# A float32 encoder trunk on one core: first two weight units by residual tile, row factors with tokens on partitions, last unit by token halves

## The chip, the cores and the metric

The kernel runs on one core of a Trainium2 chip. The metric is the device time of one execution in microseconds; where several runs are compared, their median is taken. The engines are named as in the profile: PE multiplies matrices (PEld is its loading of weights), DVE, ACT and POOL work elementwise, SP issues DMA transfers.

## The reference

A trunk of two layers on 512 tokens with 1024 features, in float32. Each layer adds four steps to the residual stream h; the mixer is a bidirectional Mamba-2 scan (SSD) in the first layer and a two-dimensional neighbourhood attention in the second.

```python
def rmsnorm(x, g):
    xf = x.astype(jnp.float32)
    y = xf * lax.rsqrt(jnp.mean(xf * xf, axis=-1, keepdims=True) + RMS_EPS)
    return (y * g.astype(jnp.float32)).astype(x.dtype)

def swiglu(x, w_gu, w_down):
    g, u = jnp.split(x @ w_gu, 2, axis=-1)
    return (jax.nn.silu(g) * u) @ w_down

for i in range(DEPTH):
    h = h + 0.5 * swiglu(rmsnorm(h, ffn1_norm[i]), ffn1_w_gu[i], ffn1_w_down[i])
    hn = rmsnorm(h, mix_norm[i])
    h = h + (ssd_mixer(hn, ...) if i % 2 == 0 else neighbourhood_attention(hn, ...))
    h = h + 0.5 * swiglu(rmsnorm(h, ffn2_norm[i]), ffn2_w_gu[i], ffn2_w_down[i])
    gate = jax.nn.sigmoid(rmsnorm(h, ple_norm[i]) @ ple_w_gate[i])
    h = h + gate * rmsnorm(p[i] @ ple_w_proj[i], ple_post_norm[i])
```

The hidden width of a feed-forward is 2816, the scan has eight groups of four heads, and the SSD mixer norms its inner 2048 features once more before its output product.

## The kernel before

**Data.** The residual lies on chip as eight tiles `h[k]` (named `hs`) of 128 features x 512 tokens, features on the partitions. Every weight matrix is cut into *units* of 128 output features: a tile `wr` of 128 x 1024. Since PE works faster on a shortened form of float32 (fp32r), each operand is split exactly into a high and a low part: `load_unit` (L149) issues a unit's transfer on SP, `split_unit` casts the high part `wh` on ACT (L157) and subtracts the low part `wl` on DVE (L159). Transfers run in the order of `plan()`, with four `wr` buffers and three of each part, so about three units stand ready ahead of use. The tiles of the residual are split likewise into pairs (`xa`, in the feed-forward after the mixer `md`): ACT L181 makes h * gain, DVE L182 its low part.

**Product.** `gemm` makes a unit's product in one PSUM bank (`ps`, 128 x 512): for each of the eight residual tiles three matmuls, high by high (L172), high by low (L173), low by high (L174), 24 in all.

**Norm.** The root-mean-square factor of a token is not applied to the input but to the product. `SumSq.add` squares a tile on ACT (L201) and adds it on POOL (L205; the eighth on DVE). `SumSq.rsqrt` multiplies the sum `acc` by a matrix of 1/1024 (L209), so that the sum over features stands on all 128 partitions, and DVE makes 1/sqrt of it on 128 x 512 (L211, then L187, L188 and three Newton steps L191 to L193) into a tile `rt`. This happens 11 times: in each layer for the two feed-forwards, the mixer, the embedding's projection and the embedding's gate, and once for the inner norm of the SSD. The calls stand behind the first unit, or the first two, that need the factor.

**Stages.** `ffn` makes gate and up units in chunks of 8, 7 and 7, each followed by `down` products of the chunk before, which add to the residual (L267); in the last `down` each finished tile is prepared for the next norm at once. In the second feed-forward `ple_proj` runs between; its `finish`, called after the third tile of the last `down`, makes a factor and scales eight tiles by it (L312). `ple` multiplies eight gate units and updates the residual (L326 to L330). In `ssd`, groups of heads are projected and scanned alternately; at its end the output products (L608, L609, L613) are scaled by the factor of the inner norm. `attention` begins with the keys.

**Order.** The instructions of each engine run in a fixed order that a scheduler made from the program when it was built. At the start of the trunk (L837 on) the constants, the eight tiles of x and the first units are issued on SP; tiles and two units are then split, and the squares counted.

Of the kernel before, what the change touches and what calls it, by code (L numbers as in the profile page):

```python
# [14 lines left out]
P = 128  # L15
T = 512
# [12 lines left out]
# columns of the packed per-partition constants  # L29
# [7 lines left out]
# columns of the shape-only constants  # L37
# [8 lines left out]
def trunk(ctx, tc, A, out):  # L46
# [45 lines left out]
    s.activation(out=warm, in_=ones_d[:, 0:1], func=AF.Silu)  # L92
# [5 lines left out]
    def park(k):  # L98
        """The residual leaves the chip while a mixer runs."""
        hd = dp.tile([P, T], F32, name=nm("hd"))  # L100
        sy.dma_start(out=hd, in_=h[k])
        h[k] = None
        return hd
# [63 lines left out]
    def gemm(pt, w, pairs, first=True, last=True, off=0):  # L167
        hi, lo = w
        n = len(pairs)
        for k, xp in enumerate(pairs):  # L170
            sl = slice((off + k) * P, (off + k + 1) * P)
            te.matmul(out=pt, lhsT=hi[:, sl], rhs=xp[:, 0, :], start=first and k == 0, stop=False)  # L172
            te.matmul(out=pt, lhsT=hi[:, sl], rhs=xp[:, 1, :], start=False, stop=False)  # L173
            te.matmul(out=pt, lhsT=lo[:, sl], rhs=xp[:, 0, :], start=False, stop=last and k == n - 1)  # L174

    def split(dst, src, gain):
        if gain is None:
            s.copy(out=dst[:, 0, :], in_=src)  # L178
            v.tensor_sub(out=dst[:, 1, :], in0=src, in1=dst[:, 0, :])
        else:  # L180
            s.activation(out=dst[:, 0, :], in_=src, func=AF.Copy, scale=gain)  # L181
            v.scalar_tensor_tensor(out=dst[:, 1, :], in0=src, scalar=gain, in1=dst[:, 0, :],  # L182
                                   op0=ALU.mult, op1=ALU.subtract)

    def newton_rsqrt(m, y, a):
        """y = 1 / sqrt(m) on VectorE: a first guess from the bits of m and three Newton steps."""
# [8 lines left out]
    class SumSq:  # L195
# [11 lines left out]
        def rsqrt(self, scale=1.0, eps=EPS):  # L207
            pt = px_bank()
            te.matmul(out=pt, lhsT=ones_d, rhs=self.acc, start=True, stop=True)  # L209
            m, a, y = sc(), sc(), rt()  # L210
            v.tensor_scalar(out=m, in0=pt, scalar1=scale, scalar2=eps, op0=ALU.mult, op1=ALU.add)  # L211
            newton_rsqrt(m, y, a)
            return y

    class Norm:
        """RMSNorm of the residual: the pairs carry h * gain, the row factor is applied after the product."""
# [7 lines left out]
        def prep(self, k, count=True):  # L224
            pr = self.alloc()
            split(pr, h[k], col(self.gain + k))
            self.pairs.append(pr)
            if count:
                self.count(k)
# [4 lines left out]
        def factor(self, half=False):  # L234
            if half:
                return self.ss.rsqrt(4.0, 4.0 * EPS)
            return self.ss.rsqrt()

# [1 line left out]
    def ffn(norm, nxt, between=lambda: None):  # L240
# [3 lines left out]
        def gate_up(f):  # L244
            pg = mm_bank()
            gemm(pg, unit(), norm.pairs)
            pu = mm_bank()
            gemm(pu, unit(), norm.pairs)
            if R[0] is None:
                R[0] = norm.factor()  # L250
# [11 lines left out]
        def down(c, finish=None):  # L262
            a, b = CHUNKS[c]
            for d in range(KD):
# [5 lines left out]
                if d == 2 and finish is not None:  # L270
                    finish()
# [14 lines left out]
    def ple_proj(l):  # L286
# [22 lines left out]
        def finish():  # L309
            r3 = ss.rsqrt(4.0, 4.0 * EPS)  # L310
# [4 lines left out]
        return pp, finish  # L315

    def ple(l, norm, pp, nxt):
        R = None
        for n in range(KD):
            pt = mm_bank()  # L320
            gemm(pt, unit(), norm.pairs)
            if R is None:
                R = norm.factor(half=True)
            u = t2()
            for cs in ((slice(0, T),) if n < KD - 1 else (slice(0, T // 2), slice(T // 2, T))):
                v.tensor_mul(out=u[:, cs], in0=pt[:, cs], in1=R[:, cs])  # L326
                s.activation(out=u[:, cs], in_=u[:, cs], func=AF.Tanh)
                v.scalar_tensor_tensor(out=u[:, cs], in0=u[:, cs], scalar=1.0, in1=pp[n][:, cs],
                                       op0=ALU.add, op1=ALU.mult)
                v.tensor_add(out=h[n][:, cs], in0=h[n][:, cs], in1=u[:, cs])  # L330
            nxt(n)

# [1 line left out]
    def ssd(norm, nxt):  # L334
# [4 lines left out]
        s.activation(out=ea, in_=ea, func=AF.Exp)  # L339
# [6 lines left out]
        R = norm.factor()  # L346
# [14 lines left out]
        def steps():  # L361
            """Step sizes, tokens on the partitions, and their running sums."""
# [6 lines left out]
            # softplus(z) = max(z, 0) + 2 atanh(e / (2 + e)), e = exp(-|z|)  # L369
# [56 lines left out]
        def project(gi):  # L426
# [3 lines left out]
            for i in range(8):  # L430
                pt = mm_bank()
                gemm(pt, unit(), norm.pairs)
# [18 lines left out]
        def scan(gi, bt, ct_, xt, zt):  # L451
            """One group of heads, in steps: what a step's products need was made in the steps before."""
            h0 = 4 * gi
            # masked C B^T of each direction, keys on the partitions
# [10 lines left out]
            # token-major xs and B  # L465
# [24 lines left out]
            def decay(hd):  # L490
                es = []
                for dr in range(2):
# [3 lines left out]
                    # the exponents of masked entries are held at 0  # L496
# [10 lines left out]
            # states carried from chunk to chunk  # L507
# [20 lines left out]
            # outputs, two heads to a tile  # L528
# [71 lines left out]
        r2 = ss.rsqrt(0.5)  # L600
        prs = pairs_of(range(8, 16), lambda: md(F32R))
        for d in range(KD):
            pt = mm_bank()
            gemm(pt, unit(), prs)
# [5 lines left out]
            # from here on tokens go column by column of the grid, so that every window of the attention is one run  # L610
# [7 lines left out]
    def attention(norm, nxt):  # L618
# [3 lines left out]
        kz = []  # L622
        R = None

        def keys(js):
            """Keys of four head pairs, normalised."""
# [3 lines left out]
            for j in js:  # L630
                pt = mm_bank()
                gemm(pt, unit(), norm.pairs)
                if R is None:
                    R = norm.factor()
# [23 lines left out]
        def stack_keys(j):  # L658
            """For each head its high parts twice over and its low parts twice over."""
# [12 lines left out]
        def stack_queries(qb):  # L672
            """For each head its high parts over its low parts, in the order of its keys' rows."""
# [14 lines left out]
        def project(j):  # L688
            """Queries and values of a head pair, in four steps."""
# [35 lines left out]
        def attend(j):  # L725
            """The four query blocks of a head pair: scores, then weights, then values, one step apart."""
# [111 lines left out]
    sy.dma_start(out=cst[:, :C_GM], in_=A["cst"][:, :C_GM])  # L838
    for k in range(KD):
        sy.dma_start(out=h[k], in_=A["x"][:, k, :])  # L840
        if k in (1, 3):
            load_unit()
# [3 lines left out]
    for k in range(KD):  # L846
        n.prep(k, False)
        if k in (1, 3):
            split_unit()
    for k in range(KD):  # L850
        n.count(k)
    for i in range(stop):
# [4 lines left out]
        if w == 0:  # L857
            ffn(n, nxt)
# [9 lines left out]
def prepare(inp):  # L868
# [62 lines left out]
    # the relative position bias laid out by query (row, column) and key (row, column)  # L931
# [29 lines left out]
```

## Time and profile before

| | us |
|---|---|
| median of 3 runs | 2466.24 |
| lowest and highest run | 2465.31, 2467.89 |
| span of the profiled execution, first to last instruction | 2462.0 |
| PE busy in it | 2395.0 (97%) |
| DVE busy | 1548.6 (63%) |
| ACT busy | 964.0 (39%) |
| POOL busy | 489.4 (20%) |

The profile shows one execution; for it the span is given, and the runs' times are those of whole executions. A row of a timeline reads: start, duration, engine, line, operation, output <- input, shape, count, and in brackets the idle time of the engine just before and what ended it. A row of the waits reads: waiting engine, tile and line, what released it, then total us, times, longest. A row of a window reads: the stretch, its length, busy time and (in brackets) instruction count of PE, PEld, DVE, ACT and POOL, then the granted clock of PE as a share of full speed, the busy share of the DMA engines and GB/s. A group of instructions reads: count, total us and mean ns of one. Starts of successive matmuls tell PE's pace; their durations overlap.

### The profile page before, as it was taken

What the parts mean: (1) busy time and instruction counts of PE and PEld (TensorE: products, weight loads), DVE (VectorE), ACT (ScalarE), POOL (GpSimd) and SP (SyncE); (2) the same over time, 40 slices, a digit from 0 to 9 for tenths busy, and PEclk for the clock granted to TensorE, in tenths of its full rate; (3) what the DMA queues carried; (4) which work ended last, traced back from release to release, by engine and by line L of the source; (5) the groups of instructions that cost most, each with busy time, mean ns of one, the idle gap of its engine ahead of it and who ended that gap; (6) DMA issues with size and microseconds to landing.
All of it is one profiled execution on the core that took longest, in us unless ns stands there. A gap on an engine that the chain in (4) does not pass through costs nothing. (4 is left out here: it accounts for less than half of the span.)

```text
span 2462.0 us, 29096 instructions
## 1 busy us (share of the span) xinstructions
PE 2395.0 (97%) x11278; PEld 1953.4 (79%) x11278; DVE 1548.6 (63%) x1983; ACT 964.0 (39%) x1545; POOL 489.4 (20%) x387
## 2 busy tenths in 40 slices
PE   8999999999999999899999999999999999999998
PEld 6888888777777778788888778888877878888887
DVE  6553448888888866645344964444478965553457
ACT  4322234555555563332234432222336753322242
POOL 2110110545555543211012111101100011110120
PEclk9999999999999999999999999999999999999999
DMA  4333342533443354233333333333434323333332
GB/s 165 96 96 100 90 126 89 167 119 122 125 123 120 122 174 129 87 101 94 96 102 95 95 93 99 99 94 92 139 120 125 112 67 99 96 94 99 99 94 77
DMA packets 89562, 266.60 MB, mean 108 GB/s; under 512 B 10944, under 2 KB 11584, under 8 KB 89424
## 3 DMA queue, kind: packets, MB, share of 16 engines
q1 hardware_dynamic: 89424, 264.75, 35.5%
q8 instruction: 88, 1.44, 0.2%
q14 instruction: 50, 0.41, 0.1%
HBM read 253.93 MB, written 10.78 MB: 108 GB/s over the span
## 5 line engine op out<-in xcount | busy, mean ns | idle before, releaser
L172 PE MATMUL ps<-xa,wh 128*128 128x512 f32 x2216 | 877.9, 396 | 17.9 <-ACT xa L181 9.2
L173 PE MATMUL ps<-xa,wh 128*128 128x512 f32 x2216 | 870.7, 393 | 3.3 <-DVE xa L182 3.3
L174 PE MATMUL ps<-xa,wl 128*128 128x512 f32 x2216 | 869.1, 392 | 0.0
L157 ACT CAST wh<-wr 128x1024 fp32r<-128x1024 f32 (+1 forms) x405 | 418.4, 1033 | 1027.2 <-PE ps L173 638.8
L159 DVE TENSOR_TENSOR wl<-wr,wh 128x1024 fp32r<-128x1024 f32 (+1 forms) x405 | 588.8, 1454 | 126.4 <-ACT wh L157 121.0
L172 PEld LDWEIGHTS ps<-xa,wh 128*128 128x128 f32 x2216 | 419.7, 189 | 108.0 <-ACT xa L181 10.6
L173 PEld LDWEIGHTS ps<-xa,wh 128*128 128x128 f32 x2216 | 419.7, 189 | 97.2 <-issue 7.1
L174 PEld LDWEIGHTS ps<-xa,wl 128*128 128x128 f32 x2216 | 418.9, 189 | 88.5 <-DVE wl L159 1.2
L172 PE MATMUL ps<-md,wh 128*128 128x512 f32 x960 | 376.6, 392 | 1.2 <-ACT md L181 1.2
L173 PE MATMUL ps<-md,wh 128*128 128x512 f32 x960 | 374.0, 390 | 1.1 <-DVE md L182 1.1
L174 PE MATMUL ps<-md,wl 128*128 128x512 f32 x960 | 373.5, 389 | 0.0
L257 POOL TENSOR_TENSOR t<-t,sc 128x512 f32<-128x512 f32 x88 | 121.2, 1379 | 1025.4 <-ACT wh L157 735.0
L205 POOL TENSOR_TENSOR sq<-sq,sq 128x512 f32<-128x512 f32 x77 | 112.0, 1454 | 595.8 <-ACT sq L201 594.6
L256 DVE TENSOR_TENSOR t<-ps,rt 128x512 f32<-128x512 f32 x88 | 60.8, 690 | 255.5 <-PE ps L174 255.5
L172 PEld LDWEIGHTS ps<-md,wh 128*128 128x128 f32 x960 | 180.2, 188 | 41.2 <-ACT md L181 2.4
L173 PEld LDWEIGHTS ps<-md,wh 128*128 128x128 f32 x960 | 180.2, 188 | 40.4 <-DVE md L182 2.3
L267 DVE SCALAR_TENSOR_TENSOR hs<-ps,hs 128x512 f32<-128x512 f32 x96 | 66.2, 690 | 229.7 <-PE ps L174 229.7
L174 PEld LDWEIGHTS ps<-md,wl 128*128 128x128 f32 x960 | 180.2, 188 | 37.6
L420 DVE SCALAR_TENSOR_TENSOR t<-t,ccw,t 128x510 f32<-128x510 f32 (+1 forms) x192 | 178.8, 934 | 5.3 <-ACT t L416 2.8
L252 DVE TENSOR_TENSOR t<-ps,rt 128x512 f32<-128x512 f32 x88 | 60.8, 691 | 127.4 <-PE ps L174 127.2
L501 POOL TENSOR_TENSOR sc<-sc,sc 128x512 f32<-128x512 f32 x64 | 106.7, 1688 | 29.8 <-ACT sc L500 29.8
L178 ACT CAST md<-t 128x512 fp32r<-128x512 f32 x88 | 54.9, 624 | 120.5 <-POOL t L257 120.5
(154 smaller groups left out, 1771.3 us busy)
## 6 DMA issues: line engine op xcount, KB each, us to landing
wr<-in_w_gu_dram SPq DMA_DIRECT2D x176, 512.0 KB, 3.6
wr<-in_w_in_dram SPq DMA_DIRECT2D x65, 512.0 KB, 3.6
wr<-in_w_dn_dram SPq DMA_DIRECT2D x64, 448.0 KB, 3.3
wr<-in_w_dn_dram SPq DMA_DIRECT2D x32, 512.0 KB, 3.5
hs<-crow SPq DMA_DIRECT2D x64, 256.0 KB, 3.6
wr<-in_w_qkv_dram SPq DMA_DIRECT2D x24, 512.0 KB, 3.6
hs<-vrow SPq DMA_DIRECT2D x64, 128.0 KB, 3.0
wr<-in_w_out_dram SPq DMA_DIRECT2D x16, 512.0 KB, 4.0
```

The lines of the kernel that those rows point to most:

```text
L157: s.copy(out=hi[:, :n], in_=raw[:, :n])
L159: v.tensor_sub(out=lo[:, :n], in0=raw[:, :n], in1=hi[:, :n])
L172: te.matmul(out=pt, lhsT=hi[:, sl], rhs=xp[:, 0, :], start=first and k == 0, stop=False)
L173: te.matmul(out=pt, lhsT=hi[:, sl], rhs=xp[:, 1, :], start=False, stop=False)
L174: te.matmul(out=pt, lhsT=lo[:, sl], rhs=xp[:, 0, :], start=False, stop=last and k == n - 1)
L205: (v if fast else g).tensor_add(out=self.acc, in0=self.acc, in1=q)
L252: v.tensor_mul(out=gm, in0=pg, in1=R[0])
L256: v.tensor_mul(out=um, in0=pu, in1=R[0])
L257: g.tensor_mul(out=um, in0=um, in1=sg)
L267: v.scalar_tensor_tensor(out=h[d], in0=pt, scalar=0.5, in1=h[d], op0=ALU.mult, op1=ALU.add)
L420: v.scalar_tensor_tensor(out=a[:, lo:hi], in0=xb[:, lo + o:hi + o], scalar=w(j), in1=a[:, lo:hi], op0=ALU.mult, op1=ALU.add)
L501: g.tensor_mul(out=e, in0=e, in1=cbm[dr])
```

## The change

*Row factor.* It is made in two parts. `begin` multiplies, for each block of 128 tokens, the squares as weights with one column of ones, so that the sums of 128 tokens stand on 128 partitions; 1/sqrt is made by DVE on 128 x 4. `end` broadcasts each column of factors as weights and multiplies it by the identity, which brings the factors into rows on all partitions, and ACT copies them to `rt`.

```diff
-        def rsqrt(self, scale=1.0, eps=EPS):
+        def begin(self, scale=1.0, eps=EPS):
             pt = px_bank()
-            te.matmul(out=pt, lhsT=ones_d, rhs=self.acc, start=True, stop=True)
-            m, a, y = sc(), sc(), rt()
-            v.tensor_scalar(out=m, in0=pt, scalar1=scale, scalar2=eps, op0=ALU.mult, op1=ALU.add)
-            newton_rsqrt(m, y, a)
-            return y
+            for c in range(NC):
+                te.matmul(out=pt[:, c:c + 1], lhsT=self.acc[:, c * P:(c + 1) * P], rhs=ones_d[:, :1],
+                          start=True, stop=True)
+            m, a, self.y = sm([NC]), sm([NC]), sm([NC])
+            v.tensor_scalar(out=m, in0=pt[:, :NC], scalar1=scale, scalar2=eps, op0=ALU.mult, op1=ALU.add)
+            newton_rsqrt(m, self.y, a)
+
+        def end(self):
+            pt = px_bank()
+            for c in range(NC):
+                te.matmul(out=pt[:, c * P:(c + 1) * P], lhsT=self.y[:, c:c + 1].to_broadcast([P, P]), rhs=ident,
+                          start=True, stop=True)
+            r = rt()
+            s.copy(out=r, in_=pt)
+            return r
```

Between the two parts lies a unit's product: in `ffn` the up unit, in `ple` the second unit (the first one's result is held in its bank till then), in `ssd` the first unit of group 0, in `attention` a second unit of keys, made ahead, in the SSD's output stage the first and second unit. `ple_proj` hands two calls to `down`, after its second and its third tile.

```diff
             pt = mm_bank()
             gemm(pt, unit(), norm.pairs)
-            if R is None:
-                R = norm.factor(half=True)
...
+            if n == 0:
+                norm.begin(half=True)
+                held = pt
+                continue
+            if n == 1:
+                R = norm.end()
+                gate(0, held, R, slice(0, T))
+                nxt(0)
```

*Start.* The constants and, in halves of 512 columns, the first two units are issued on ACT's queue; the halves are cast behind tile 0 and tile 3. The first feed-forward's gate and up products go side by side, residual tile by tile. All squares come after the last cast of a residual tile. The table of the exponential for the SSD's decay rates is used later (`ea` is kept in program order).

```diff
+    sy.dma_start(out=h[0], in_=A["x"][:, 0, :])
+    s.dma_start(out=cst[:, :C_GM], in_=A["cst"][:, :C_GM])
+    for x in range(2):
+        for src, raw, hi, lo in begun:
+            s.dma_start(out=raw[:, wcols[x]], in_=src[:, wcols[x]])
+    s.activation(out=warm, in_=ones_d[:, 0:1], func=AF.Silu)
...
     for k in range(KD):
         n.prep(k, False)
-        if k in (1, 3):
-            split_unit()
-    for k in range(KD):
-        n.count(k)
+        if k in (0, 3):
+            for src, raw, hi, lo in begun:
+                sl = wcols[k // 3]
+                s.copy(out=hi[:, sl], in_=raw[:, sl])
+                last_lo = v.tensor_sub(out=lo[:, sl], in0=raw[:, sl], in1=hi[:, sl])
+
+    def first(pg, pu, pairs):
+        for k in range(KD):
+            for pt, (src, raw, hi, lo) in zip((pg, pu), begun):
+                gemm(pt, (hi, lo), pairs[k:k + 1], first=k == 0, last=k == KD - 1, off=k)
+
+        with tc.issue_after(n.last_cast.ins):
+            for k in range(KD):
+                n.count(k)
```

*Tail.* The last gate unit of the last layer is multiplied in two halves of 256 tokens, each in a bank of its own; each half is gated and its residual stored at once, one on SP's queue and one on ACT's. Before, one product was gated in two halves.

```diff
+            if n == KD - 1 and nxt is done:
+                w = unit()
+                for x, cs in enumerate(halves):
+                    pt = mm_bank()
+                    gemm(pt[:, cs], w, norm.pairs, cols=cs)
+                    gate(n, pt[:, cs], R, cs)
+                    (sy, s)[x].dma_start(out=out[:, n, cs], in_=h[n][:, cs])
+                continue
```

How the change moves instructions, at three places. In the changed kernel `gemm` has the lines 171 to 173, the casts are at L156 and L921, their subtractions at L158, the tiles' casts at L180 and L181, `begin` at L211 and L214, `end` at L221 and L224; `ps_140` is the gate's and `ps_141` the up unit's bank.

PE at the start of the program, before (the first rows, and those where the second unit begins):

```order
L172 MATMUL ps_159<-xa_100,wh_108 128x512
L173 MATMUL ps_159<-xa_100,wh_108 128x512
L174 MATMUL ps_159<-xa_100,wl_110 128x512
...
L172 MATMUL ps_159<-xa_124,wh_108 128x512
L172 MATMUL ps_190<-xa_100,wh_120 128x512
L173 MATMUL ps_190<-xa_100,wh_120 128x512
L173 MATMUL ps_159<-xa_124,wh_108 128x512
```

and after the change:

```order
L171 MATMUL ps_140<-xa_108,wh_83 128x512
L172 MATMUL ps_140<-xa_108,wh_83 128x512
L173 MATMUL ps_140<-xa_108,wl_84 128x512
L171 MATMUL ps_141<-xa_108,wh_86 128x512
L172 MATMUL ps_141<-xa_108,wh_86 128x512
L173 MATMUL ps_141<-xa_108,wl_87 128x512
L171 MATMUL ps_140<-xa_115,wh_83 128x512
```

The first bank was filled nearly to its end before the second one began; now the two alternate with every residual tile.

PE at the end of these two units in the changed kernel (`sq_190` is the sum of squares, `sm_220` the factors, `ps_250` the third unit's bank):

```order
L173 MATMUL ps_141<-xa_137,wl_87 128x512
L211 MATMUL ps_213<-ones_d,sq_190 128x1 x4
...
L171 MATMUL ps_250<-xa_134,wh_253 128x512
L221 MATMUL ps_233<-msk,sm_220 128x128 x4
L172 MATMUL ps_250<-xa_134,wh_253 128x512
```

The first part of the factor stands behind both units, the second part inside the third.

DVE where the last `down` of the first layer's second feed-forward meets the embedding's projection, before (`hs` with L267 is a residual tile's update, L182 its low part, L312 the scaling):

```order
L267 SCALAR_TENSOR_TENSOR hs_7679<-ps_10183,hs_7679 128x512
L192 SCALAR_TENSOR_TENSOR sc_10126<-sc_10126,sc_10125 128x512
L159 TENSOR_TENSOR wl_10223<-wr_10089,wh_10221 128x896
L193 SCALAR_TENSOR_TENSOR rt_10127<-sc_10126,rt_10127 128x512
L182 SCALAR_TENSOR_TENSOR md_10212<-hs_7679,cst,md_10212 128x512
L312 SCALAR_TENSOR_TENSOR xa_9929<-xa_9929,cst,rt_10127 128x512 x2
L312 SCALAR_TENSOR_TENSOR xa_9951<-xa_9951,cst,rt_10127 128x512 x2
L312 SCALAR_TENSOR_TENSOR xa_9980<-xa_9980,cst,rt_10127 128x512 x2
L312 SCALAR_TENSOR_TENSOR xa_10003<-xa_10003,cst,rt_10127 128x512 x2
L267 SCALAR_TENSOR_TENSOR hs_7723<-ps_10218,hs_7723 128x512
L159 TENSOR_TENSOR wl_10258<-wr_10149,wh_10256 128x1024
L182 SCALAR_TENSOR_TENSOR md_10247<-hs_7723,cst,md_10247 128x512
```

and after, from the last Newton step of the factor on (L290 is the update, L335 the scaling):

```order
L191 TENSOR_TENSOR sm_10138<-sm_10139 128x4
L192 SCALAR_TENSOR_TENSOR sm_10138<-sm_10138,sm_10137 128x4
L193 SCALAR_TENSOR_TENSOR sm_10139<-sm_10138,sm_10139 128x4
L290 SCALAR_TENSOR_TENSOR hs_7656<-ps_10152,hs_7656 128x512
L158 TENSOR_TENSOR wl_10207<-wr_10098,wh_10205 128x896
L181 SCALAR_TENSOR_TENSOR md_10181<-hs_7656,cst,md_10181 128x512
L335 SCALAR_TENSOR_TENSOR xa_9973<-xa_9973,cst,rt_10192 128x512 x2
L335 SCALAR_TENSOR_TENSOR xa_9995<-xa_9995,cst,rt_10192 128x512 x2
L335 SCALAR_TENSOR_TENSOR xa_10024<-xa_10024,cst,rt_10192 128x512 x2
L335 SCALAR_TENSOR_TENSOR xa_10047<-xa_10047,cst,rt_10192 128x512 x2
L290 SCALAR_TENSOR_TENSOR hs_7700<-ps_10202,hs_7700 128x512
L158 TENSOR_TENSOR wl_10242<-wr_10153,wh_10240 128x896
```

The scaling stood behind the low part of `hs_7679` and stands one tile earlier now (`hs_7700` answers to `hs_7679` of before); the factor's operations have 128x4 elements instead of 128x512 and stand closer together.

117 lines of the change are left out of this document (75 added, 42 removed).

## The prediction

> **What bounds the kernel now.** I read the page's table of engines first, then the waits of PE, then the timeline at each place that the change touches.
>
> ```profile
> span 2462.0 us, 29096 instructions
> PE 2395.0 (97%) x11278; PEld 1953.4 (79%) x11278; DVE 1548.6 (63%) x1983; ACT 964.0 (39%) x1545; POOL 489.4 (20%) x387
> PE ps L556 <- DVE md L526: 23.0, 14, 2.0
> ...
> PE ps L172 <- ACT xa L181: 9.2, 4, 4.5
> PE ps L172 <- ACT wh L157: 8.7, 1, 8.7
> PE ps L173 <- DVE xa L182: 3.3, 5, 1.3
> PE ps L172 <- ACT md L181: 1.2, 2, 0.6
> PE ps L173 <- DVE md L182: 1.1, 2, 0.5
> ```
>
> PE is busy 97% of the span, so a change gains only where it takes matmul time away or closes one of PE's gaps. The waits name the gaps. The largest, 23.0 us, lies inside the groups of the SSD scan, whose instructions the change leaves in their order (so does a second one there, on POOL). The rest is at the start (8.7 us before the first matmul, 3.3 us at L173) and where one stage hands over to the next (9.2, 1.2 and 1.1 us). The change can win there, some 15 us at most, and it pays for it with more instructions on PE.
>
> **The row factor.** It is made 11 times. Before, one fp32 matmul of the all-ones matrix with the squares (L209) gives the sum to all partitions, and twelve DVE operations run on 128x512.
>
> ```profile
> 380.44 1.02 PE L209 MATMUL ps<-sq,ones_d 128*128 128x512 f32 x2
> ...
> 381.53 0.39 PE L173 MATMUL ps<-xa,wh 128*128 128x512 f32 x1
> 381.76 0.40 PE L174 MATMUL ps<-xa,wl 128*128 128x512 f32 x1
> 1881.75 1.09 PE ps L711 x8
> L711 PE MATMUL ps<-msk,sc 128*128 128x128 f32 x64 | 8.7, 279 | 0.0
> L366 PE MATMUL ps<-msk,t x4: 222/222/272, 397.8 to 398.0; 64*128 64x64 f32 x4
> L209 PEld LDWEIGHTS ps<-sq,ones_d 128*128 128x128 f32 x22 | 4.0, 188 | 1.4 <-PE ps L173 0.4 <-DVE sq L205 0.3
> ```
>
> Steady matmuls start .23 us apart (381.53, 381.76). L209 starts at 380.44 and the second matmul behind it at 381.53: 1.09 less one matmul's .23 is .86 us of PE that goes. In its place come two pieces. The second piece (four matmuls with a column of factors broadcast as weights and the identity streamed, eight instructions, since fp32 runs as two) has its match in L711, also fp32 with 128 columns and a load for each: eight last 1.09, the last one's .28 of it is pipeline tail, so (1.09 - .28)/7 = .116 each, .9 for the piece. The first piece (the squares as weights, a single column streamed, again eight) has no match. Its matmuls are next to nothing, its eight weight loads are all. From below: the four loads and matmuls of L366 lie within .2 us, about .06 each, and eight with a gap of .1 make .6. From above: a load that nothing hides takes .19 in L209's row, and eight make 1.5. I take .75, close to the low end, because L366 shows loads running into each other. One factor then costs PE .75 + .9 - .86 = +.8 us (+.65 to +1.55; +.3 if loads hide under the matmuls ahead, as nearly all of today's do, and only .25 of the first piece shows). The start's factor is counted with the start, and that of the SSD's inner norm hides in a loop that PE doesn't bound (below): nine count, **+7.1 us** (+2.7 to +14).
>
> The Trainium skill, in "TensorE: Matmul & The Clock Gate", section "LDWEIGHTS (loading the stationary operand)", gives a load as its column count over 1.2 in ns, 107 ns for 128 columns. Eight would be .86 and the nine factors +8.1; L366's rows, at about .06 each, speak for less. By the page the sum would be -.7.
>
> On DVE twelve operations shrink:
>
> ```profile
> L193 DVE SCALAR_TENSOR_TENSOR rt<-sc,rt 128x512 f32<-128x512 f32 x33 | 25.0, 758 | 1.0
> L193 DVE SCALAR_TENSOR_TENSOR sm<-sm,sm 128x8 f32<-128x8 f32 x24 | 3.9, 160 | 0.2
> ```
>
> From about .7 to about .16 each: some 8 us of DVE per factor become 2, and ACT gets one copy of 128x512. At 63% and 39% neither engine bounds the whole, so this is worth nothing by itself. It matters where DVE's queue is behind.
>
> **Feed-forward to embedding (both layers).** Here it is behind: the ple_proj factor's chain and the eight scalings stand in DVE's queue ahead of the last residual tiles.
>
> ```profile
> 1361.17 5.38 DVE L312 SCALAR_TENSOR_TENSOR xa<-xa,cst,rt 128x512 f32<-128x512 f32 x8
> ...
> 1372.81 0.68 DVE L267 SCALAR_TENSOR_TENSOR hs<-ps,hs 128x512 f32<-128x512 f32 x1
> 1373.28 0.40 PE L174 MATMUL ps<-md,wl 128*128 128x512 f32 x1
> 1374.30 0.50 PE L172 MATMUL ps<-md,wh 128*128 128x512 f32 x1 [0.63 <-ACT md L181]
> 1375.34 0.50 PE L173 MATMUL ps<-md,wh 128*128 128x512 f32 x1 [0.54 <-DVE md L182]
> ```
>
> From 1373.28 to 1374.30 and on to 1375.34 two starts take 2.06 where .46 would do: PE loses 1.6. The scalings stay, a tile earlier, and with the 6 us that leave the chain the backlog clears. **-3.2 us** for both layers. If the last tile's own chain (its update at 1372.81, then cast and low part) is what PE waits for, nothing is gained.
>
> **Embedding to the next layer.** Once only.
>
> ```profile
> 1417.06 0.75 DVE L326 TENSOR_TENSOR t<-ps,rt 128x256 f32<-128x256 f32 x2
> 1419.56 0.39 PE L174 MATMUL ps<-xa,wl 128*128 128x512 f32 x1
> 1421.55 0.50 PE L172 MATMUL ps<-xa,wh 128*128 128x512 f32 x1 [1.60 <-ACT xa L181]
> 1422.34 0.50 PE L173 MATMUL ps<-xa,wh 128*128 128x512 f32 x1 [0.28 <-DVE xa L182]
> 1423.40:1426.80 3.40, 3.40 (x10) 2.64 (x9) 1.23 (x1) 0.56 (x1) 0.00 (x0) 0.50 0.24 31
> ```
>
> From 1419.56 to 1422.34 two starts take 2.78 for .46: PE waits 2.3 us for the last tile of the residual. Right behind, the granted clock is .50 for 3.4 us, in which 10 matmuls start where 15 would: 3.4 us of work at half pace, another 1.7 (here and below: half the stretch). 1419.56 is the 21st matmul of the new stage (the tiles before the last), so its first ran at 1419.56 - 20 x .228 = 1415.0, and the embedding's last bank was full then. L326 took it up at 1417.06, 2 us late: DVE still carries the backlog that the factor's twelve operations left at the head of this stage. With 6 us less of them L326 starts with its bank. I expect a remainder of .6 us and no half clock: **-3.4 us** (-4 if nothing is left; 0 if the chain from L326 to the cast, 1417.06 to 1421.55, grows longer by what else then gets ahead of it on DVE).
>
> **The start.**
>
> ```profile
> 2.12 0.43 SPq L149 DMA_DIRECT2D wr<-in_w_gu_dram  x1
> ...
> 7.65 1.04 ACT L157 CAST wh<-wr 128x1024 fp32r<-128x1024 f32 x1 [0.89 <-DMA wr<-in_w_gu_dram]
> ...
> 11.03 0.63 PE L173 MATMUL ps<-xa,wh 128*128 128x512 f32 x1
> 11.45 0.63 PE L174 MATMUL ps<-xa,wl 128*128 128x512 f32 x1
> ...
> 13.57 1.33 ACT L181 ACTIVATE xa<-hs,cst 128x512 fp32r<-128x512 f32 x2
> ...
> 13.81 5.25 POOL L205 TENSOR_TENSOR sq<-sq,sq 128x512 f32<-128x512 f32 x3 [0.36 <-ACT sq L201]
> 25.94 1.02 PE L209 MATMUL ps<-sq,ones_d 128*128 128x512 f32 x2
> 8.75:25.94 17.19, 14.38 (x48) 10.23 (x49) 14.68 (x13) 9.72 (x16) 8.48 (x5) 1.00 0.73 267
> 969.74 1.29 POOL L205 TENSOR_TENSOR sq<-sq,sq 128x512 f32<-128x512 f32 x1 [2.59 <-ACT sq L201]
> ```
>
> The first two units' 48 matmuls take 17.19 us, though at .23 they need 10.9: a dozen start .42 apart (11.03, 11.45), and PE waits for one residual tile after another (3.3 us in the waits). After the change each tile feeds six matmuls instead of three, and the halves of the weights are cast before the later tiles. A whole unit took from its issue at 2.12 to its cast at 7.65; the first half, issued about a microsecond sooner and half as long, I let land at 6.5, and with its cast PE starts at about 7.3. With .42 each until 12.4 and .23 behind, 48 matmuls end at about 20.6. But the squares now stand behind the last weight cast: ACT has eight casts of residual tiles (.67 each, 13.57's row) and four half casts (.52) before them, 7.4 us from about 6 on, and reaches them at about 13.5. POOL adds six at 1.29 from 14.5 on, and DVE's last add ends near 22.6. So PE waits some 2 us at the factor's first piece; queued behind it on PE is the third unit, which needs no factor. The second piece lies inside that unit, with 4.3 us of matmuls ahead of it; DVE needs 2 for the factor and its queue puts two weight subtractions of a microsecond or more among them, so PE may wait another .4 there. The third unit ends at about 30.3 (22.6 + .75 + 5.47 + .9 + .4, rounded up); before, 25.94 + .86 + 5.47 = 32.3. That is -1.9. A gap of 2.3 brought half clock above, so I put three chances in ten on another 1.7: **-1.4 us** (-4 if the adds keep up; +3 if POOL runs at the 1.75 of 13.81's row, 5.25 for three, and a half clock follows).
>
> On that half clock the Trainium skill, same page, "Part 1: The HAM clock gate", has the clock drop after an idle window of about 3.4 us; by that, 2 us cost nothing more. The rows at 1421.55 and 1423.40 show a drop after less than that.
>
> **The SSD's inner norm.**
>
> ```profile
> 963.68 0.69 DVE L608 TENSOR_TENSOR t<-ps,md 128x512 f32<-128x512 f32 x1
> 969.78 0.68 DVE L608 TENSOR_TENSOR t<-ps,md 128x512 f32<-128x512 f32 x1
> ```
>
> The output loop turns every 6.1 us where PE needs 5.47 for a unit, so POOL and DVE set its pace and the factor hides; the first unit now runs while the factor is made: **-.5 us**. The first two units of the SSD and of the attention are handled the same way and cost only their factors.
>
> **The tail.**
>
> ```profile
> 2456.28 0.76 DVE L326 TENSOR_TENSOR t<-ps,rt 128x256 f32<-128x256 f32 x2 [2.63 <-PE ps L174]
> ```
>
> The last unit becomes 48 matmuls of 256 columns, at .116 or so for L711's 128 fp32 columns, the same streaming: about 5.6 instead of 5.45. The chain behind its last matmul, which now runs both halves through each operation (.76 for two), then has only one: some -.5. Net **-.3 us**.
>
> **Sum:** 7.1 - 3.2 - 3.4 - 1.4 - .5 - .3 = -1.7, 2460.3 for a span of 2462.0. The median of the runs is 2466.24, 4.2 above that span, which the change doesn't touch: **2464.5 us**. The runs shown differ by 2.6 (2465.31 to 2467.89); I call no change what lies within 0.2%, 4.9 us, either side.
>
> **Rivals.** (1) *The loads hide under the matmuls ahead* and each factor costs +.3: nine are +2.7 in place of 7.1, and the sum is -6.1; with another us at the start, 2459. For it: weight loads are busy 79% of the span beside a PE at 97%, so nearly all are hidden today. Against: seven of the eight have only a one-column matmul to hide under. (2) *Each one-column matmul waits for its own load* of .19: +14 in place of +7.1, a sum of +5.2, 2471.5. It decides from .15 a load on. For it is the load's 188 ns; against it L711's .116 with a load of its own each. (3) *The hand-overs stay*, since the last residual tile's own chain sets them and not the backlog: -6.6 becomes about -1, the sum +3.9, 2470. The rows at 1372.81 to 1374.30 (update, cast, PE) leave little slack between them, which speaks for it; the row of 5.38 just ahead speaks against. (4) *The adds on POOL are late at the start*: +3 in place of -1.4, 2469. The shared pace of 1.75 speaks for it.
> One thing more moves all of these: in the SSD scan there are stretches at half clock, as
>
> ```profile
> 464.30:471.10 6.80, 5.84 (x18) 4.97 (x19) 6.80 (x10) 4.83 (x12) 2.63 (x2) 0.50 0.40 118
> ```
>
> and if the scan starts a us or two sooner there may be one more or one less, some 2.7 us each way.
>
> **How the numbers follow.** The forecast has .42, with a range of its own of 2461 to 2469; rival 1 .32, rival 2 .10, rival 3 .10, rival 4 .06. Faster than 2461.3: most of rival 1 (.30) and a lower corner of the forecast (.08), together .38. Slower than 2471.2: half of rivals 2 and 3 (.10) and what the scan's half clocks and rival 4 add (.07), together .17. The rest, .45, is no change. The range from 2455 (rival 1 with all gaps closed and one half clock less) to 2473 (rival 2 with one more) leaves out about 2 in 10.
>
> **What would show it.** Right: eight one-column matmuls at .06 to .1 each, the piece with the identity in .9; first matmul near 7.3 and a wait of about 2 us ahead of the first factor; no wait over .3 us where the embedding's first unit meets its last tiles; clock 1.00 at the start of the second layer; DVE's total some 65 us lower with the end nearly unmoved. Wrong: factors above 2.5 us on PE, the brackets of 1374.30 and 1421.55 still there, a new wait at a factor's second piece, or half-clock stretches in the SSD in another number.

## The result and the profile after

The changed kernel takes 2486.81 us (median of 5 runs, 2484.24 to 2491.37) against 2466.24 us (5 runs, 2465.31 to 2468.17): the ratio is 1.0082, with a 95% interval of 1.0069 to 1.0094. It is 20.6 us slower. The forecast was 2464.5 with a range of 2455 to 2473, so the time lies outside it, and no rival reached it either.

The page of the changed kernel (its span and its engines) and the waits of PE show that most of what was forecast about waits did happen:

```profile
span 2482.4 us, 29485 instructions
PE 2421.4 (98%) x11456; PEld 1971.5 (79%) x11456; DVE 1483.0 (60%) x1985; ACT 967.9 (39%) x1556; POOL 489.6 (20%) x387
PE ps L171 <- ACT wh L921: 7.2, 1, 7.2
PE ps L171 <- ACT xa L180: 5.6, 2, 4.5
PE ps L518 <- DVE sc L510: 3.8, 1, 3.8
PE ps L211 <- DVE sq L205: 2.8, 1, 2.8
...
PE ps L221 <- DVE sm L193: 0.4, 2, 0.2
PE ps L172 <- DVE xa L181: 0.3, 1, 0.3
```

The first matmul comes at 7.2 (it was 8.75), the waits for `md` at the embedding's gate (1.2 and 1.1 before) are gone from the list, those for `xa` fell from 9.2 and 3.3 to 5.6 and 0.3, and DVE works 65.6 us less. The new wait at the first factor (2.8) is the one that was foreseen as 2. One wait inside the SSD scan, L518 (L470 before), grew from 1.2 to 3.8. In all PE waits less and the span is 20.4 us longer: PE's busy time grew by 26.4, from 2395.0 to 2421.4. The factors' new matmuls were forecast at 9 us of that (eleven at .8). So other matmuls take longer too. Windows of 40 us, first of the kernel before, then two of the changed one (PE's busy time with the number of matmuls in brackets comes first, the granted clock is the last but two):

```profile
300.00:340.00 40.00, 40.00 (x178) 33.14 (x177) 15.89 (x18) 8.20 (x9) 2.08 (x1) 1.00 0.32 93
```

```profile
100.00:140.00 40.00, 40.00 (x178) 33.11 (x177) 20.22 (x18) 11.44 (x14) 5.16 (x4) 1.00 0.31 96
300.00:340.00 40.00, 40.00 (x173) 32.19 (x172) 15.72 (x19) 8.32 (x10) 2.18 (x1) 1.00 0.32 92
```

PE has no gap in any of the three and its clock is full, but between 300 and 340 the changed kernel does 173 matmuls where 178 were done before, and where it still does 178 between 100 and 140. Their starts are 229 and 238 ns apart in turn, 233 in the mean, instead of 227. From 100 to 140 the moving tiles are `xa` (gate and up units), from 300 to 340 `md` (down units). Through the whole trace the slow pace holds wherever weights meet streamed `md` tiles (the three `down` stages of each feed-forward, the second half of the SSD's output products, the attention's output, the embedding's gate), 2856 matmuls of 512 columns, and not where `xa` is. (The pairs of the residual are `md` ahead of the embedding's gate, and not in the feed-forward after the mixer.) Over `md` the starts are 233.0 ns apart in the mean, and 226.9 in the kernel before; over `xa` they are 227.2 and 227.1 (starts further apart than 262 ns left out). Summed over the matmuls, what lies above 226.7 ns is 17.8 us over `md` and 3.1 over `xa` in the changed kernel, and .4 and 2.6 in the one before.

No line of the change alters these matmuls. What moved is where `md` lies. A pool gives each kind of tile its place in the order of first use, and the small tiles `sm` (12 of 32 bytes per partition) were first used in the attention, behind `md`; now the first factor uses them, ahead of `md`. In the built programs `md` begins at byte 162208 before and at 162592 after, 384 bytes on, while weights and `xa` stay.

### The profile page after: what moved, and what is told of

The parts are those of the page before. It is cut to its first block, busy times and chain, and to the rows that moved or that the text cites. A ratio compares the mean times of both kernels' runs of the same rounds, so it can differ in the third digit from the quotient of the medians.

```text
span 2482.4 us, 29485 instructions
## 1 busy us (share of the span) xinstructions
PE 2421.4 (98%) x11456; PEld 1971.5 (79%) x11456; DVE 1483.0 (60%) x1985; ACT 967.9 (39%) x1556; POOL 489.6 (20%) x387
## 4 chain that ended last, share of the span: by engine, by line
PE 87%; DVE 7%; ACT 2%; issue 2%; POOL 1%; DMA 1%; SPq 0%; POOLq 0%; DVEq 0%; ACTq 0%
PE ps L171 27%; PE ps L172 27%; PE ps L173 27%; DVE t L465 3%; DVE wl L158 1%; PE ps L604 1%; PE ps L840 1%; DVE md L573 1%; PE ps L797 1%; PE ps L587 1%; POOL t L663 1%; POOL sq L205 1%; PE ps L518 1%; DVE md L469 1%; PE ps L831 1%
## 5 line engine op out<-in xcount | busy, mean ns | idle before, releaser
L156 ACT CAST wh<-wr 128x1024 fp32r<-128x1024 f32 (+1 forms) x403 | 415.7, 1032 | 1033.7 <-PE ps L172 603.2
L158 DVE TENSOR_TENSOR wl<-wr,wh 128x1024 fp32r<-128x1024 f32 (+1 forms) x403 | 587.0, 1457 | 122.2 <-ACT wh L156 110.5
L171 PE MATMUL ps<-md,wh 128*128 128x512 f32 (+1 forms) x968 | 381.9, 394 | 0.0
L172 PE MATMUL ps<-md,wh 128*128 128x512 f32 (+1 forms) x968 | 380.5, 393 | 0.0
L173 PE MATMUL ps<-md,wl 128*128 128x512 f32 (+1 forms) x968 | 380.3, 393 | 0.0
L290 DVE SCALAR_TENSOR_TENSOR hs<-ps,hs 128x512 f32<-128x512 f32 x96 | 66.4, 691 | 250.4 <-PE ps L173 250.4
L465 DVE SCALAR_TENSOR_TENSOR t<-t,ccw,t 128x510 f32<-128x510 f32 x192 | 179.6, 936 | 6.4 <-ACT t L461 3.7
```

The lines of the kernel that those rows point to most:

```text
L156: s.copy(out=hi[:, :n], in_=raw[:, :n])
L158: v.tensor_sub(out=lo[:, :n], in0=raw[:, :n], in1=hi[:, :n])
L171: te.matmul(out=pt, lhsT=hi[:, sl], rhs=xp[:, 0, cols], start=first and k == 0, stop=False)
L172: te.matmul(out=pt, lhsT=hi[:, sl], rhs=xp[:, 1, cols], start=False, stop=False)
L173: te.matmul(out=pt, lhsT=lo[:, sl], rhs=xp[:, 0, cols], start=False, stop=last and k == n - 1)
L290: v.scalar_tensor_tensor(out=h[d], in0=pt, scalar=0.5, in1=h[d], op0=ALU.mult, op1=ALU.add)
```

## The experiments

**Is it the place of md, or the factor's short matmuls?** First the changed kernel with `sm` in a pool behind all others, which puts `md` back:

```diff
+    sp = ctx.enter_context(tc.tile_pool(name="sp", bufs=1))
...
     def sm(shape, dt=F32):
-        return bp.tile([P] + list(shape), dt, name=nm("sm"), tag="sm", bufs=12)
+        return sp.tile([P] + list(shape), dt, name=nm("sm"), tag="sm", bufs=12)
```

> The changed kernel, with the small tiles of the factor (sm) in a pool of their own behind all others, so that the md tiles lie at the address that they had before the change (162208 instead of 162592 bytes). Nothing else differs. Theory P (placement): in the changed kernel the matmuls that stream md tiles start every 233 ns instead of 227, from the 384 bytes by which md moved; here they go back to 227, and the time falls by 16 to 20 us, to 2467 to 2471. Rival F (the factor's new short matmuls throw PE's pipeline out of step and the slow pace lasts on): the 233 ns stay, 2484 to 2491.

Measured: 2471.33 us (10 runs, 2466.68 to 2472.23), 1.0016 of the kernel before (1.0007 to 1.0025). Then the other way round, the kernel before with `md` moved:

```diff
     for k in range(KD):
         n.count(k)
+    v.memset(sm([8]), 0.0)
```

> The kernel before the change, with one sm tile allocated ahead of the md tiles (and set to zero), so that md moves by 384 bytes to where the changed kernel has it. P: matmuls over md at 233 ns, the time rises by 16 to 20 us, to 2482 to 2487. F: no change, 2464 to 2468.

Measured: 2481.15 us (4 runs, 2477.70 to 2483.01), 1.0056 (1.0040 to 1.0073) of the kernel before, 2466.21 beside it. And the kernel before with everything moved by the same 384 bytes:

```diff
+    pad = cp.tile([P, 96], F32, name="pad")
+    v.memset(pad, 0.0)
     cst = cp.tile([P, C_N], F32, name="cst")
```

> The kernel before the change, with an unused constant tile of 384 bytes ahead of everything, so that weights, xa and md all move by 384 bytes and keep their distances. If what counts is the distance between the moving tile and the weights, modulo something, no change: 2464 to 2468, all paces 227. If the address itself counts, all 9500 matmuls of 512 columns go to 233 ns: about 63 us more, 2529.

Measured: 2466.54 us (10 runs), 1.0003 (0.9994 to 1.0012). The same window of the three kernels, in this order, has

```profile
300.00:340.00 40.00, 40.00 (x178) 33.13 (x177) 15.95 (x18) 8.19 (x9) 2.13 (x1) 1.00 0.32 92
```

```profile
300.00:340.00 40.00, 40.00 (x173) 32.23 (x172) 14.97 (x18) 8.41 (x10) 2.17 (x1) 1.00 0.32 93
```

```profile
300.00:340.00 40.00, 40.00 (x178) 33.15 (x177) 15.21 (x18) 8.20 (x9) 1.39 (x1) 1.00 0.33 95
```

178, 173 and 178 matmuls: placement alone makes the slow pace and takes it away, with the new factor and without it. Rival F falls on both sides. Undoing it is worth 15.5 us (2486.81 to 2471.33), making it costs 14.9 (10 to 18 by the interval). Both are a little under the 16 to 20 that P expected and far from F's nothing. And since moving everything together costs nothing, it is the distance between the moving tile and the weights that counts and not the address.

**Which distances are slow?** A program of matmuls alone, 48 for each distance, on one core with nothing beside them, in one profiled execution:

```python
for k in range(8):
    w = slice(wo + P * k, wo + P * (k + 1))
    for i, (a, o) in enumerate(((W, 0), (W, T), (L, 0))):
        te.matmul(out=acc, lhsT=a[:, w], rhs=X[:, xo + o:xo + o + T],
                  start=k == 0 and i == 0, stop=k == 7 and i == 2)
```

> Only matmuls, 48 for each placement, in the pattern of the kernel (weights high, high, low; moving high, low, high): the moving tile is shifted from the weights by 0 to 512 bytes in steps of 32, then by 640 to 2048, then the weights are shifted under a moving tile at 384. Everything else of the computation is left out; the output is not the reference's. P: 227 ns at shift 0 and 2048, 233 at 384, and a pattern that tells which shifts are slow; with the weights shifted by 384 too, 227 again. F: 227 throughout, since no short matmul is in it.

First and last matmul of the blocks with the moving tile shifted by 0, 64, 256 and 384 bytes, and of the one with both shifted by 384, from its timeline:

```profile
35.04 0.39 PE L71 MATMUL acc<-X,W 128*128 128x512 f32 x1
...
45.70 0.39 PE L71 MATMUL acc<-X,L 128*128 128x512 f32 x1
...
57.13 0.40 PE L71 MATMUL acc<-X,W 128*128 128x512 f32 x1
...
67.89 0.39 PE L71 MATMUL acc<-X,L 128*128 128x512 f32 x1
...
124.16 0.40 PE L71 MATMUL acc<-X,W 128*128 128x512 f32 x1
...
134.82 0.39 PE L71 MATMUL acc<-X,L 128*128 128x512 f32 x1
...
168.46 0.40 PE L71 MATMUL acc<-X,W 128*128 128x512 f32 x1
...
179.43 0.39 PE L71 MATMUL acc<-X,L 128*128 128x512 f32 x1
...
345.13 0.39 PE L71 MATMUL acc<-X,W 128*128 128x512 f32 x1
...
355.79 0.40 PE L71 MATMUL acc<-X,L 128*128 128x512 f32 x1
```

47 steps lie between the first and the last start: (45.70 - 35.04)/47 is 226.8 ns, and the others come to 228.9, 226.8, 233.4 and 226.8. The mean distance of starts in all blocks (the first six of each left out):

| shift of the moving tile against the weights, bytes | ns from start to start |
|---|---|
| 0, 256, 512, 768, 1024, 1280, 1536, 1792, 2048 | 226.6 to 226.7 |
| 64, 320 | 228.8 |
| 32, 96, 128, 192, 224, 288, 352, 384, 448, 480, 640, 896 | 233.3 to 233.4 |
| 160, 416 | 234.2 |
| moving tile at 384, weights at 128 / 384 / 896 (distance a multiple of 256) | 226.9 / 226.7 / 226.7 |
| moving tile at 384, weights at 0 / 256 / 512 | 233.4 / 232.4 / 232.4 |

A matmul of 128x512 in fp32r runs at its fast pace when the distance of its two operands is a multiple of 256 bytes, and loses 2 to 8 ns otherwise. Only multiples of 32 bytes were tried. The slow pace itself moves by a ns with the place of the weights (the last row). In the kernel before, all lists of tiles between the weights and `md` are multiples of 2048 bytes long, so weights, `xa` and `md` happened to lie at such distances.

The rule was then put to the whole kernel, by nothing but the number of small tiles in the changed kernel (12):

```diff
-        return bp.tile([P] + list(shape), dt, name=nm("sm"), tag="sm", bufs=12)
+        return bp.tile([P] + list(shape), dt, name=nm("sm"), tag="sm", bufs=16)
```

> The changed kernel with one number changed: 16 small tiles instead of 12, so that md moves by 512 bytes in all and not 384. By the rule of m1_offsets (shifts of a multiple of 256 bytes are fast) md's matmuls go back to 227 ns and the time to that of e1_sm_last, 2467 to 2472. If any move of md from its old address is slow: 2484 or more.

> The changed kernel with 10 small tiles, so that md moves by 320 bytes, 64 more than a multiple of 256. By m1_offsets (228.8 ns at 64 and 320) the matmuls over md lose 2.1 ns each instead of 6.6: a third of the loss, 5 to 6 us above e5_sm16, 2473 to 2478. If only the multiple of 256 counts: 2484 or more.

Measured: 2471.72 us with 16 tiles (10 runs, 2467.37 to 2474.98; ratio 1.0020, 1.0011 to 1.0029) and 2478.08 with 10 (4 runs, 2476.95 to 2479.61; 1.0046, 1.0033 to 1.0060). The window from 300 to 340 holds 178 and 177 matmuls:

```profile
300.00:340.00 40.00, 40.00 (x178) 33.15 (x177) 16.48 (x19) 8.70 (x10) 2.17 (x1) 1.00 0.32 92
```

```profile
300.00:340.00 40.00, 40.00 (x177) 32.81 (x176) 16.38 (x19) 8.60 (x10) 2.18 (x1) 1.00 0.32 92
```

The second is 6.4 us slower than the first where the rule gave 5 to 6; the 2484 or more of the two other readings did not come.

**What is left: the change without its accident.** With `md` in place the change is still 5.1 us slower than before, where 1.7 faster was forecast. The factor alone and the start alone, each put into the kernel before (`md` in place):

> The kernel before with the new row factor at all its eleven places and md at its old address; start and last unit as before the change. Theory T (each factor costs PE .8 us as forecast, the hand-overs give 6 us back, and the SSD's output stage, where the second part of the factor waits for a whole unit, loses 2 instead of gaining .5): +7.1 - 3.2 - 3.4 + 2 = +2.5, 2468.7 (2466 to 2471). Rival U (what is left over in e1_sm_last is a higher price of every factor on PE, some 1.4 us): 2473 or more.

> The kernel before with the new start alone (halved first units on ACT's queue, products side by side, squares after the last cast); the factor by one matrix of ones and the last unit as before. T: -1.5, 2464.7 (2462 to 2467), the first factor's wait for the squares taking most of what the earlier matmuls gain. U says nothing of it.

Measured: the factor 2472.32 us (7 runs, 2468.31 to 2473.34; 1.0026, 1.0015 to 1.0037), the start 2463.89 (11 runs, 2462.39 to 2466.13; 0.9991, 0.9983 to 1.0000). So the start gives its 1.5 and more, as T said, and the factor loses 5.9, over twice T's 2.5 and just short of U's 2473. U's price of 1.4 a factor is not found either: it is .93. Its price on PE is read in the changed kernel around the embedding's gate, at the first and the second part:

```profile
1387.10 0.95 PE L211 MATMUL ps<-ones_d,sq 128*128 128x1 f32 x8
1387.91 0.48 PE L171 MATMUL ps<-md,wh 128*128 128x512 f32 x1
1388.22 0.39 PE L172 MATMUL ps<-md,wh 128*128 128x512 f32 x1
...
1393.57 1.05 PE L221 MATMUL ps<-msk,sm 128*128 128x128 f32 x8
1394.38 0.48 PE L171 MATMUL ps<-md,wh 128*128 128x512 f32 x1
1394.70 0.40 PE L172 MATMUL ps<-md,wh 128*128 128x512 f32 x1
```

Counted as L209 was (to the second matmul behind, less one matmul of .23) the first part costs 1.12 - .23 = .89 us and the second 1.13 - .23 = .90, together .93 more than the .86 that went. L366, by which the prediction sized the first part, is no match for it:

```profile
L366 PEld LDWEIGHTS ps<-msk,t x4: 135/138/140, 397.8 to 397.9; 64*128 64x128 f32 x4
```

Its loads have 128 columns too, but they belong to transposes and stand on 64 partitions instead of 128. Which of the two makes them quicker was not tried.

Matched matmul by matmul with the kernel of e3_all_384 (the kernel before in a profiled execution with a like row of half-clock stretches), f1_factor loses .93 at each of the eleven factors and about .5 more at each `ple_proj` (PE waits for `sm` there, 0.4 us for two in the list of waits above, and then starts late), and wins 1.9 at each feed-forward's hand-over to the embedding and 2.0 at the embedding's to the next layer: 10.2 + 1.0 - 3.8 - 2.0 = 5.4. The rest, to 6.5 between the two spans (2470.4 and 2463.9), lies ahead of the first matmul (.9) and around the end of the SSD, where half-clock stretches fall differently.

The SSD's output stage was the suspect for that rest:

```diff
+        r2 = ss.rsqrt(0.5)
         prs = pairs_of(range(8, 16), lambda: md(F32R))
-        pts = [mm_bank()]
-        gemm(pts[0], unit(), prs)
-        ss.begin(0.5)
         for d in range(KD):
-            if d < KD - 1:
-                pts.append(mm_bank())
-                gemm(pts[-1], unit(), prs)
-            if d == 0:
-                r2 = ss.end()
-            pt = pts.pop(0)
+            pt = mm_bank()
+            gemm(pt, unit(), prs)
```

> As e1_sm_last, with the factor of the SSD's inner norm made as before (one matrix of ones, ahead of the output products). T: POOL's first scaling comes 1.4 us earlier and the stage costs .85 us less on PE: 2 us less than e1_sm_last, 2469 (2467 to 2471), and between the first output product and the next stage as long as in the kernel before. U: .6 less at most.

Measured: 2471.26 us (11 runs, 2466.74 to 2472.42; 1.0017, 1.0008 to 1.0025) beside e1_sm_last's 2471.33. T's point falls, as a loss of 2 is not seen; the intervals are too wide to tell a gain of .5 from nothing. The traces tell more. Matched matmul by matmul, f4_r2_old gains .94 on e1_sm_last at the stage's first units (at 961 us), the price of one factor, and loses it again behind them, where its half-clock stretch lasts 13.7 us and e1_sm_last's 10.2. So the new factor cost its price there too and did not hide.

**A selection.** Kernels that keep what paid: the new start, the last unit by halves, the two-part factor only where DVE's backlog held PE up (and, in the first of them, for the first factor), `md` in place. In the first one the start's factor stands behind the third unit.

> A selection: the new start with its factor made a unit pair later (behind the third unit), the new factor only for the embeddings (projection and gate), the old one elsewhere, the last unit by halves, md at its old address. T: hand-overs -6.6, four factors +3.2 (and the first's .8), start -4 with the wait for the squares gone, tail -.5: about -7, 2459 (2455 to 2463). U: 2463 or more.

Measured: 2463.11 us (11 runs, 2460.13 to 2466.80; 0.9989, 0.9980 to 0.9998), 3.3 us under the kernel before beside it: half of the gain that was expected, and just inside U's side of the border. The wait for the squares is gone, but PE stops in the third unit instead, for the low part of a weight:

```profile
24.58 0.50 PE L174 MATMUL ps<-xa,wl 128*128 128x512 f32 x1 [2.28 <-DVE wl L159]
```

Matched with f2_start, what b1_selected is ahead at the third unit (2.7 us) is gone one unit later. The second one went further:

```diff
-            r3 = ss.end()
+            r3 = ss.rsqrt(4.0, 4.0 * EPS) if l else ss.end()
...
-            if first and R[0] is None:
-                norm.begin()
             pu = mm_bank()
...
-                R[0] = norm.end() if first else norm.factor()
+                R[0] = norm.factor()
```

> As b1_selected, but the first factor by the matrix of ones, behind the fourth unit, and the new factor only in the first layer's embedding, where the next feed-forward follows. By the traces of f1_factor and b1_selected a factor in two parts costs PE .95 more than the old one, the embedding's first hand-over returns 1.9 a layer and its last 2.0 in the first layer alone: 1 to 2 us less than b1_selected, 2461.5 (2459 to 2464). If b1_selected's gain came from the two-part factors, it is slower than b1_selected, 2464 or more.

Measured: 2470.03 us (11 runs, 2467.95 to 2473.21; 1.0012, 1.0003 to 1.0021), 7 us slower than b1_selected. The timeline of PE names the place:

```profile
47.36 0.76 PE L172 MATMUL ps<-xa,wh 128*128 128x512 f32 x1 [5.71 <-DVE t L292]
47.92 0.63 PE L173 MATMUL ps<-xa,wh 128*128 128x512 f32 x1
48.35 0.63 PE L174 MATMUL ps<-xa,wl 128*128 128x512 f32 x1
```

The five product banks were full of units that waited for the factor, and the long DVE chain of the old factor came too late to empty one; PE stood for 5.7 us and went on at half clock (starts .43 apart). That it was this and not the second layer was tried by putting the factor back behind the first two units:

```diff
                 first(pg, pu, norm.pairs)
-                held.append((f, pg, pu))
+                R[0] = norm.factor()
+                gated(f, pg, pu)
                 return
```

> As b2_layer0, with the first factor (matrix of ones) right behind the first two units again, as in f2_start: PE no longer runs out of the five product banks, on which it waited 5.9 us at 47 in b2_layer0. If that wait and the half clock behind it are what b2_layer0 lost, 2462 (2460 to 2464): f2_start's 2463.9, less 1.5 for the first layer's embedding. If the loss came from the old factor in the second layer, 2468 or more.

Measured: 2462.45 us (11 runs, 2458.61 to 2465.06; 0.9981, 0.9972 to 0.9990). It is the fastest here, 4.6 us under the kernel before and 24 under the changed one.

## Why the prediction was wrong, point by point

- **The step that failed** is in the sum: it added what the edited places gain and lose and took for granted that every other matmul keeps the pace of "Steady matmuls start .23 us apart". The change moved `md` by 384 bytes against the weights, and its matmuls then started 6.1 ns further apart in the mean: 14.9 us when this alone was done to the kernel before, 15.5 less when it alone was undone. No view of the profile before could show it, and the comparison of orders names tiles, not addresses; but the first use of `sm` did move from behind `md` to ahead of it, which the diff shows.
- **The factor's size** was off: .93 us a piece on PE where .8 was taken, since the one-column matmuls cost .89 (.111 each) and not .75. The row they were sized by, L366, is of another kind (transposes on 64 partitions), and its .06 a load did not carry over. The Trainium skill, in "TensorE: Matmul & The Clock Gate", section "LDWEIGHTS (loading the stationary operand)", gives a load as its column count over 1.2 in ns, 107 ns for 128 columns. The first piece, at .111 a load, is near that; L366's loads are not. Rival 2 (.19 a load) is excluded, rival 1 (hidden loads) too. With the tenth factor, the SSD's inner one, which didn't hide, and the 1.0 lost at the two `ple_proj`, the term is 10 x .93 + 1.0, +10.3 instead of +7.1.
- **The hand-over to the embedding**: forecast -3.2 for both layers, found -3.8. The wait went with DVE's backlog, as said, and rival 3 falls. Whether the shorter chain did it or the scalings' earlier place was not tried apart.
- **The hand-over to the next layer**: forecast -3.4, found -2.0. The wait went as forecast, but the half clock behind it, 1.7 of the 3.4, was an accident of the execution that was profiled: e3_all_384, which has the same order of work, shows none there (below), nor do e2_md_384 and f2_start.
- **The start**: forecast -1.4; -2.5 in f2_start. First matmul at 7.2 for 7.3, the wait for the squares 2.8 for 2. With the new factor in it less is left: e1_sm_last, which has the start and the tail beside the factor, is 1.0 us under f1_factor. Matched matmul by matmul it leads f1_factor by 2.5 us at the third unit and by .9 one unit later, behind a half-clock stretch at 24 us. The prediction gave that stretch three chances in ten; of the seven profiled executions that wait at the first factor, five have it.
- **The SSD's inner norm**: forecast -.5; no gain found (f4_r2_old against e1_sm_last: .1 in the medians), but the factor's price of .94 in the traces. **The tail**: forecast -.3; from the last unit's start on, e1_sm_last's span ends .6 us sooner against f1_factor's.

With `md` in place the terms come to 10.3 - 3.8 - 2.0 - 1.6 (f2_start's 2.5 less .9 for its factor) - .6 = +2.3 for the change; e1_sm_last measured +5.1, with an interval of 1.7 to 6.2. The difference goes with the clock. Ahead of the last 20 us, e1_sm_last's trace has 47.8 us at half clock and the kernel before 37.5, and half of the difference is 5.1 us. The mean granted clock of eight of e1_sm_last's ten runs is .990; the two at .991 took 2466.68 and 2467.10 us, as long as the kernel before took at .991 (15 runs, 2464.49 to 2468.20). How much of this the change brings about itself, by its wait at the first factor, stays open.

## What to carry to other kernels

Compare where tiles lie, not only in what order instructions run: a small tile that is first used earlier can shift every tile behind it, and then work that nobody touched changes its pace. Keep the operands of long runs of fp32r matmuls a multiple of 256 bytes apart (a pool of their own for odd-sized tiles does it). Size a new instruction by a row of the same shape and kind, or call the term open. And before a stall's after-effect in one profile is counted as a gain, look whether another execution of the same work has it too.

## What the runs showed of the hardware

For fp32r matmuls of 128x512, each with weights of its own, the pace of a PE without any gap depends on the distance of its two operands in memory, modulo 256 bytes: 226.7 ns at 0, 228.8 at 64, 232 to 234 at the other multiples of 32 that were tried. Why was not tried.

Stretches at half clock come and go from one execution to the next. The windows of e3_all_384 at the end of the SSD and behind the hand-over to the second layer, where the profile before had a clock of .50 (its hand-over is 3.5 us later, at 1425.04):

```profile
888.30:895.10 6.80, 5.74 (x15) 4.59 (x16) 5.49 (x8) 5.46 (x8) 0.00 (x0) 0.50 0.99 335
1426.90:1430.30 3.40, 3.40 (x16) 2.80 (x15) 1.23 (x1) 0.56 (x1) 0.00 (x0) 1.00 0.08 20
```

The profile before has no stretch at 888 and one at 1423, behind its hand-over. A wait of 3.5 us of e1_sm_last at the first factor was followed by 3.4 us at .50, one of 2.8 of the changed kernel at the same place by none:

```profile
24.05:27.46 3.41, 3.41 (x10) 2.81 (x11) 3.16 (x8) 0.00 (x0) 0.00 (x0) 0.50 0.54 157
```

```profile
24.05:27.46 3.41, 3.41 (x19) 2.94 (x20) 3.37 (x7) 0.00 (x0) 0.00 (x0) 1.00 0.43 142
```

The length of the wait alone does not decide it: in f4_r2_old a wait of 2.1 at that place was followed by 6.8 us at .50, and in f2_start one of 3.0 by none.

```profile
23.70:30.50 6.80, 6.80 (x20) 5.62 (x20) 4.82 (x15) 0.00 (x0) 0.00 (x0) 0.50 0.63 195
```

This is likely also why the runs of one kernel here spread by several us. The mean granted clock of a run falls as its time rises: the changed kernel's five runs took 2484.24 us at .992, 2484.33 and 2486.81 at .991, 2488.98 at .990 and 2491.37 at .989. By an estimate, .003 less over 2485 us is 15 us at half clock, some 7 us of time, and the runs differ by 7.1. That is a correlation; no run sets the stretches on purpose.
